# Row sums of a 64 MiB matrix on one core: which rows the first and the last loads of a partition take

## The chip, the core and the metric

The kernel runs on one core of a Trainium2 chip. The metric is the device time of one execution in microseconds, as the median of several runs; lower is better. The profile is of one further execution, and its span begins at the first instruction and ends with the last.

## The reference

```python
batch, seq, dim = 32, 512, 1024
x = np.random.randn(batch, seq, dim).astype(np.float32)

def reference(x):
    return np.sum(x, axis=-1).astype(np.float32)
```

There are 16,384 rows of 1,024 floats (4 KB each), and each row gives one float: 67.1 MB are read, and 64 KB are written.

## The kernel before

Each of the 128 partitions sums J = 128 rows. The rows of the matrix are cut in two regions. `x_a` is the first 2,048 rows, of which partition p takes the 16 rows from 16p on (64 KB from one partition to the next). `x_b` is the other 14,336 rows, of which partition p takes the 112 rows from 2048 + 112p on (448 KB from one partition to the next). The sums stand in one tile `sums` of 128 columns: columns 0 to 111 belong to `x_b`, columns 112 to 127 to `x_a`. `rows_from(j, n)` gives the n rows that belong to the columns from j on, for all partitions. Each load has 128 contiguous runs, one for each partition.

All loads are issued by SyncE in one queue, in this order: a first load of 7 rows for each partition (columns 0 to 6, from `x_b`); seven whole loads of 16 rows, of which the first takes `x_a` (columns 112 to 127) and the six others take `x_b` from column 16 on; then the last 9 rows (columns 7 to 15, from `x_b`) in pieces of 6 rows, 2 rows, 560 floats and 464 floats of the last row. The tiles come from a pool of three buffers, so that a load waits until the reduction of the third tile before it has been done. The first load's instruction is moved to the very start of the program (`issue_first_load_at_entry`). The second load waits until a small ScalarE instruction (`ready`) is over, and the third until the first reduction is done.

VectorE reduces the first load and six whole tiles with one `tensor_reduce` each (line 152). The last whole tile and the pieces are shared between VectorE (`halves`, line 166, which adds the two halves of a row and accumulates) and ScalarE (line 179). At the end ScalarE's queue stores the columns 16 to 111 and the columns 112 to 127 in two DMAs; both wait for the load of the 2 rows. SyncE stores the columns 0 to 15 when the last row is summed. All three stores are issued in line 202, and the end of the program waits for them.

Of the kernel before, what the change touches and what calls it, by code (L numbers as in the profile page):

```python
# [100 lines left out]
@with_exitstack  # L101
def kernel(
    ctx: ExitStack,
    tc: tile.TileContext,
    x: bass.AP,
    out: bass.AP,
):
    nc = tc.nc
    nc.at_finalize(issue_first_load_at_entry)
    nc.at_finalize(order_waits)  # L110
    nc.at_finalize(wait_for_the_store_at_the_clear)
    fp32 = mybir.dt.float32
    P = 128
    batch, seq, dim = x.shape
    rows = batch * seq
    J = rows // P
    BIG = 16

    LONG = J - BIG
    rows_in = x.flatten_outer_dims()
    rows_out = out.rearrange("b s -> (b s)")
    x_a = rows_in[: P * BIG].rearrange("(p j) d -> p j d", p=P)
    x_b = rows_in[P * BIG :].rearrange("(p j) d -> p j d", p=P)
    out_a = rows_out[: P * BIG].rearrange("(p j) -> p j", p=P)
    out_b = rows_out[P * BIG :].rearrange("(p j) -> p j", p=P)


    def rows_from(j, n):
        return x_b[:, j : j + n, :] if j < LONG else x_a[:, j - LONG : j - LONG + n, :]

    last = 0
    FIRST = 7
    pieces = (560, 464)
    LINE = 64

    with (
        tc.tile_pool(name="small", bufs=1) as smallpool,  # L140
        tc.tile_pool(name="in", bufs=3) as inpool,
        tc.tile_pool(name="unread", bufs=4, space=bass.MemoryType.PSUM) as upool,
        tc.tile_pool(name="stage", bufs=1) as stpool,
        tc.manual_schedule(),
    ):


        seed = smallpool.tile([P, LINE // 2], fp32)
        sums = stpool.tile([P, J], fp32)

        def vec(dst, src):
            return nc.vector.tensor_reduce(  # L152
                out=dst, in_=src, axis=mybir.AxisListType.X, op=mybir.AluOpType.add
            )

        def hold(inst, until, reason):
            tc.add_manual_dep(
                inst.ins,
                until.ins.name,
                mybir.DependencyInfo(mybir.DependencyClass.Sync, mybir.DependencyReason.DATA),  # L160
                reason=reason,
            )

        def halves(dst, src):
            n = src.shape[-1] // 2
            return nc.vector.tensor_tensor_reduce(  # L166
                out=src[:, :n],
                in0=src[:, :n],
                in1=src[:, n:],
                scale=1.0,  # L170
                scalar=0.0,
                op0=mybir.AluOpType.add,
                op1=mybir.AluOpType.add,
                accum_out=dst,
            )

        def act(dst, src, n):
            unread = upool.tile([P, dim], fp32)
            nc.scalar.activation(  # L179
                out=unread[:, :n],  # L180
                in_=src,
                func=mybir.ActivationFunctionType.Copy,
                accum_out=dst,
            )

        sums_of = []

        def rows(t, a, n, j, n_act, pairs=False):
            nv = n - n_act
            block = t[:, a * dim : (a + n) * dim].rearrange("p (n d) -> p n d", d=dim)  # L190
            load = nc.sync.dma_start(out=block, in_=rows_from(j, n))  # L191
            if pairs:
                for q in range(nv):
                    sums_of.append(halves(sums[:, j + q : j + q + 1], block[:, q, :]))
            else:
                sums_of.append(vec(sums[:, j : j + nv], block[:, :nv, :]))
            for q in range(nv, n):
                act(sums[:, j + q : j + q + 1], block[:, q, :], dim)
            return load

        def store(eng, dst, j0, j1):
            return eng.dma_start(out=dst, in_=sums[:, j0:j1])

        nc.vector.memset(seed[:, :1], 0.0)  # L204
        unread = upool.tile([P, dim], fp32)
        ready = nc.scalar.activation(  # L206
            out=unread[:, :1], in_=seed[:, :1], func=mybir.ActivationFunctionType.Copy
        )

        j = last  # L210
        t = inpool.tile([P, BIG * dim + LINE], fp32)
        rows(t, 0, FIRST, j, 0)
        first = sums_of[-1]
        wholes = [LONG, *range(BIG, LONG, BIG)]
        for k, at in enumerate(wholes):
            t = inpool.tile([P, BIG * dim + LINE], fp32)
            if k < len(wholes) - 1:
                load = rows(t, 0, BIG, at, 0)
            else:
                rows(t, 0, BIG, at, 7, pairs=True)  # L220
            if k == 0:
                hold(load, ready, "no second load while the first one's descriptors are made")
            if k == 1:
                hold(load, first, "no descriptors of later loads while the first ones start")

        t = inpool.tile([P, BIG * dim + LINE], fp32)
        rows(t, FIRST, 6, j + FIRST, 2, pairs=True)
        two = rows(t, FIRST + 6, 2, j + FIRST + 6, 1, pairs=True)
        a = BIG - 1

        j += a
        c, width = pieces
        whole = t[:, a * dim + c : BIG * dim + 2]
        nc.vector.memset(whole[:, width + 1 :], 0.0)  # L234
        part = t[:, a * dim : a * dim + c]
        nc.sync.dma_start(out=part, in_=rows_from(j, 1)[:, 0, :c])  # L236
        nc.sync.dma_start(out=whole[:, :width], in_=rows_from(j, 1)[:, 0, c:])
        late = "its packets come behind those of the loads"
        hold(store(nc.scalar, out_b[:, BIG:], BIG, LONG), two, late)
        hold(store(nc.scalar, out_a, LONG, J), two, late)  # L240
        halves(whole[:, width : width + 1], part)
        halves(sums[:, j : j + 1], whole)
        store(nc.sync, out_b[:, :BIG], 0, BIG)


# [28 lines left out]
```

## Time and profile before

| what | us |
|---|---|
| median of 3 runs (161.13 to 161.27) | 161.14 |
| span of the profiled execution | 159.5 |
| first load (7 rows) landed | 11.0 |
| one whole tile (16 rows), from landing to landing | 19.3 |
| its `tensor_reduce` on VectorE | 17.2 |
| last piece landed | 157.3 |
| last store issued | 157.8 |

The profiled execution's own time is not listed apart from its span; the median of the runs stands 1.6 us above that span, for what lies around it. The table's times are read from the chain of waits, in order of time, and from the timeline: a reduction starts when its load has landed, so the starts of the reductions give the landings.

### The profile page before, as it was taken

To read this page: it belongs to the slowest core of one execution; us is meant where nothing else is said; L and a number is where in the kernel's file an instruction comes from. 1 tells how busy PE (TensorE), PEld (TensorE's weight loads), DVE (VectorE), ACT (ScalarE), POOL (GpSimd) and SP (SyncE) were. 2 spreads that over 40 slices of the span, in tenths; PEclk is the share of its full clock that TensorE was granted. 3 is DMA by queue.
4 is the path that set the end of the run, shared out by engine and by line. 5 is a ranking of instruction groups with operands and counts; after the bars stand their busy time and mean duration, and the time that the engine had idled before them with its cause. 6 is when DMAs were issued, how large, how long until landed. Compare 5 with 4: busy or idle time off the path is not lost.

```text
span 159.5 us, 135 instructions
## 1 busy us (share of the span) xinstructions
DVE 120.6 (76%) x41; ACT 12.1 (8%) x22; POOL 0.2 (0%) x4
## 2 busy tenths in 40 slices
DVE  0029600499995999769996899949999499994955
ACT  3000000000000000000000000000000000003993
POOL 0000000000000000000000000000000000000000
DMA  8899899699699699699699798996996996996993
GB/s 302 388 493 526 362 427 526 296 493 526 263 526 526 263 526 526 263 526 493 296 526 444 345 526 378 411 526 296 493 526 263 526 526 263 526 526 265 425 382 128
DMA packets 2160, 67.18 MB, mean 421 GB/s; under 512 B 624, under 2 KB 752, under 8 KB 880
## 3 DMA queue, kind: packets, MB, share of 16 engines
q1 hardware_dynamic: 1872, 67.12, 97.8%
q10 hardware_dynamic: 288, 0.06, 0.2%
HBM read 67.11 MB, written 0.07 MB: 421 GB/s over the span
## 4 chain that ended last, share of the span: by engine, by line
DMA 71%; DVE 27%; SPq 1%; issue 0%; DVEq 0%
DMA t<-in_x_dram 71%; DVE sums L152 26%; SPq L191 0%; SPq L236 0%; DVE t L166 0%; DVEq L269 0%
## 5 line engine op out<-in xcount | busy, mean ns | idle before, releaser
L152 DVE TENSOR_REDUCE sums<-t 128x16 f32<-128x16384 f32 (+1 forms) x7 | 110.9, 15849 | 32.3 <-DMA t<-in_x_dram 32.3
L179 ACT ACTIVATE unread<-t 128x1024 f32<-128x1024 f32 x10 | 10.1, 1011 | 144.3 <-DMA t<-in_x_dram 144.3
L166 DVE CUSTOM_DVE_ANT_0 t<-t 128x512 f32<-128x512 f32 (+2 forms) x16 | 9.6, 654 | 4.0 <-DMA t<-in_x_dram 4.0
L179 ACT ACTIVATION_READ_ACCUMULATOR unread<-t 128x1 f32 x10 | 1.9, 188 | 0.0
L206 ACT ACT_TABLE_LOAD x1 | 1.3, 1283 | 0.8 <-PEq L258 0.8
L166 DVE DVE_READ_ACCUMULATOR2_ANT sums<- 128x1 f32 x15 | 1.2, 82 | 0.0
L204 DVE MEMSET seed<- 128x1 f32 x1 | 0.1, 59 | 0.8 <-PEq L258 0.8
L206 ACT ACTIVATE unread<-seed 128x1 f32<-128x1 f32 x1 | 0.2, 174 | 0.0
L258 POOL MEMSET const-bfloat16-1.0<- 128x1 bf16 x1 | 0.1, 102 | 0.0
L258 POOL MEMSET const-uint8-127<- 128x1 uint8 x1 | 0.1, 102 | 0.0
L258 POOL MEMSET const-float32-0.0<- 128x1 f32 x1 | 0.1, 99 | 0.2 <-issue 0.2
L258 POOL MEMSET const-float32-1.0<- 128x1 f32 x1 | 0.1, 99 | 0.0
L166 DVE DVE_READ_ACCUMULATOR2_ANT t<- 128x1 f32 x1 | 0.1, 83 | 0.0
L234 DVE MEMSET t<- 128x1 f32 x1 | 0.1, 59 | 0.0
## 6 DMA issues: line engine op xcount, KB each, us to landing
t<-in_x_dram SPq DMA_DIRECT2D x1, 3584.0 KB, 11.0
t<-in_x_dram SPq DMA_DIRECT2D x1, 3072.0 KB, 28.7
t<-in_x_dram SPq DMA_DIRECT2D x1, 1024.0 KB, 30.7
t<-in_x_dram SPq DMA_DIRECT2D x1, 280.0 KB, 31.0
t<-in_x_dram SPq DMA_DIRECT2D x1, 232.0 KB, 31.1
t<-in_x_dram SPq DMA_DIRECT2D x7, 40.7
out_dram<-sums ACTq DMA_DIRECT2D x1, 48.0 KB, 1.6
out_dram<-sums ACTq DMA_DIRECT2D x1, 8.0 KB, 1.6
```

Source lines behind the costliest of these rows:

```text
L152: return nc.vector.tensor_reduce(out=dst, in_=src, axis=mybir.AxisListType.X, op=mybir.AluOpType.add)
L166: return nc.vector.tensor_tensor_reduce(out=src[:, :n], in0=src[:, :n], in1=src[:, n:], scale=1.0, scalar=0.0, op0=mybir.AluOpType.add, op ...
L179: nc.scalar.activation(out=unread[:, :n], in_=src, func=mybir.ActivationFunctionType.Copy, accum_out=dst,)
L204: nc.vector.memset(seed[:, :1], 0.0)
L206: ready = nc.scalar.activation(out=unread[:, :1], in_=seed[:, :1], func=mybir.ActivationFunctionType.Copy)
L234: nc.vector.memset(whole[:, width + 1 :], 0.0)
L258: nc = _bacc.Bacc("TRN2", target_bir_lowering=False, num_devices=1)
```

## The change

The 16-row region and the 112-row region stay the same rows of the matrix, but other columns and other loads take them. Columns 0 to 15, which are the first load of 7 rows and the last 9 rows, now come from the 16-row region (`near`), and columns 16 to 127, which are the seven whole loads, all come from the 112-row region (`far`). Within the 16-row region, partition 4q+b takes the block of 16 rows with the number 32b+q (before it was partition p and block p). So the partitions 4q, 4q+1, 4q+2 and 4q+3 read blocks 2 MiB apart, and partition 4q+4 reads the block next to that of partition 4q. In the DMA the source of such a load has two counting dimensions (q of 32, then b of 4) and a contiguous run.

The stores follow the loads. ScalarE's queue issues one store of the columns 16 to 127 in place of two, 448 contiguous bytes of each partition, back to back in memory. SyncE's last store writes the columns 0 to 15 as 64-byte runs that together fill 8 KB, in the same order of blocks as the loads; before, its 64-byte runs were 448 bytes apart. The load's target is now written as one contiguous stretch of the tile's row instead of as rows of 1,024.

```diff
-    LONG = J - BIG
+    SPREAD = 4
     rows_in = x.flatten_outer_dims()
     rows_out = out.rearrange("b s -> (b s)")
-    x_a = rows_in[: P * BIG].rearrange("(p j) d -> p j d", p=P)
-    x_b = rows_in[P * BIG :].rearrange("(p j) d -> p j d", p=P)
-    out_a = rows_out[: P * BIG].rearrange("(p j) -> p j", p=P)
-    out_b = rows_out[P * BIG :].rearrange("(p j) -> p j", p=P)
+    near = rows_in[: P * BIG].rearrange("(b q j) d -> q b (j d)", b=SPREAD, j=BIG)
+    far = rows_in[P * BIG :].rearrange("(p j) d -> p (j d)", p=P)
+    out_near = rows_out[: P * BIG].rearrange("(b q j) -> q b j", b=SPREAD, j=BIG)
+    out_far = rows_out[P * BIG :].rearrange("(p j) -> p j", p=P)
+
+    def cols_from(j, c, n):
+        at = j * dim + c
+        return near[:, :, at : at + n] if j < BIG else far[:, at - BIG * dim : at - BIG * dim + n]
 
     def rows_from(j, n):
-        return x_b[:, j : j + n, :] if j < LONG else x_a[:, j - LONG : j - LONG + n, :]
+        return cols_from(j, 0, n * dim)
...
-            load = nc.sync.dma_start(out=block, in_=rows_from(j, n))
+            load = nc.sync.dma_start(out=t[:, a * dim : (a + n) * dim], in_=rows_from(j, n))
...
-        wholes = [LONG, *range(BIG, LONG, BIG)]
+        wholes = range(BIG, J, BIG)
...
-        nc.sync.dma_start(out=part, in_=rows_from(j, 1)[:, 0, :c])
-        nc.sync.dma_start(out=whole[:, :width], in_=rows_from(j, 1)[:, 0, c:])
+        nc.sync.dma_start(out=part, in_=cols_from(j, 0, c))
+        nc.sync.dma_start(out=whole[:, :width], in_=cols_from(j, c, width))
         late = "its packets come behind those of the loads"
-        hold(store(nc.scalar, out_b[:, BIG:], BIG, LONG), two, late)
-        hold(store(nc.scalar, out_a, LONG, J), two, late)
+        hold(store(nc.scalar, out_far, BIG, J), two, late)
         halves(whole[:, width : width + 1], part)
         halves(sums[:, j : j + 1], whole)
-        store(nc.sync, out_b[:, :BIG], 0, BIG)
+        store(nc.sync, out_near, 0, BIG)
```

## The prediction

> **What bounds the kernel now.** I read the page first. Its first line gives the span, and its strip of slices shows the DMA engines busy from the first slice to nearly the last, while VectorE has holes.
>
> ```profile
> span 159.5 us, 135 instructions
> DVE 120.6 (76%) x41; ACT 12.1 (8%) x22; POOL 0.2 (0%) x4
> q1 hardware_dynamic: 1872, 67.12, 97.8%
> HBM read 67.11 MB, written 0.07 MB: 421 GB/s over the span
> ```
>
> The load queue alone holds 97.8% of the 16 engines' time. Next I asked how steady that is: the busy time by windows, each lying inside one whole load.
>
> ```profile
> core 0: us, DVE busy (x) ACT busy (x) POOL busy (x), PEclk, DMA share, GB/s
> 12.00:29.00 17.00, 6.65 (x1) 0.00 (x0) 0.00 (x0) 1.00 1.00 432
> 31.00:48.00 17.00, 16.52 (x1) 0.00 (x0) 0.00 (x0) 1.00 1.00 432
> 128.00:145.00 17.00, 16.12 (x1) 0.00 (x0) 0.00 (x0) 1.00 1.00 432
> ```
>
> The DMA share is 1.00 and the rate 432 GB/s in each of them. The first of these windows reads the 16-row region (64 KB from partition to partition), the others the 112-row region (448 KB); both go at one rate. Only what stands before and after this stream is left to win or lose, so I read the timeline there.
>
> ```profile
> 11.03 7.62 DVE L152 TENSOR_REDUCE sums<-t 128x7 f32<-128x7168 f32 x1 [10.14 <-DMA t<-in_x_dram]
> 30.30 17.22 DVE L152 TENSOR_REDUCE sums<-t 128x16 f32<-128x16384 f32 x1 [11.65 <-DMA t<-in_x_dram]
> 49.62 17.22 DVE L152 TENSOR_REDUCE sums<-t 128x16 f32<-128x16384 f32 x1 [2.10 <-DMA t<-in_x_dram]
> ...
> 146.28 0.69 DVE L166 CUSTOM_DVE_ANT_0 t<-t 128x512 f32<-128x512 f32 x1 [2.16 <-DMA t<-in_x_dram]
> ...
> 156.05 0.94 ACTq L202 DMA_DIRECT2D out_dram<-sums  x2
> ...
> 157.32 0.40 DVE L166 CUSTOM_DVE_ANT_0 t<-t 128x233 f32<-128x233 f32 x1 [0.19 <-DMA t<-in_x_dram]
> 157.65 0.08 DVE L166 DVE_READ_ACCUMULATOR2_ANT sums<- 128x1 f32 x1
> 157.76 0.35 SPq L202 DMA_DIRECT2D out_dram<-sums  x1
> ```
>
> From 30.30 to 146.28 six whole loads of the 112-row region land: 115.98 / 96 = 1.208 us a row. The load of the 16-row region takes 30.30 - 11.03 = 19.27 us, 1.204 a row. VectorE always waits for a landing, some 2.1 us before each tile, so it is never what is late. The first landing is at 11.01 in the chain of waits, where 7 rows at the stream's pace are 8.46: **2.55 us are start**. The 9 last rows take 157.32 - 146.28 = 11.04, against 10.87 at that pace: 0.17 are pieces. From the last landing (157.30) to the end of the span (159.49) 2.19 us pass: the last sum (0.42 with its read-out), the store and the close of the program. The issues by DMA say how long a store takes.
>
> ```profile
> t<-in_x_dram SPq DMA_DIRECT2D x1, 3584.0 KB, 11.0
> out_dram<-sums ACTq DMA_DIRECT2D x1, 48.0 KB, 1.6
> out_dram<-sums ACTq DMA_DIRECT2D x1, 8.0 KB, 1.6
> out_dram<-sums SPq DMA_DIRECT2D x1, 8.0 KB, 1.4
> ```
>
> So before is: start 2.55 + 112 rows at 1.208 (135.30) + 16 rows at 1.204 (19.26) + pieces 0.17 + end 2.19 = 159.47, against 159.49. The median of the runs, 161.14, is 1.65 above that span, and I keep 1.65 for the time around it.
>
> **The change, part by part.**
>
> *The rows that trade places.* The seven whole loads now all read the 112-row region at 1.208: that region still has 112 rows, so 135.30 again. The 16 rows of the other region are now the first 7 and the last 9. Their bytes and runs (28, 24, 8, 2.2 and 1.9 KB for a partition) are as before; only the addresses differ. Nearest line: the same region at 432 GB/s and 1.204. I keep 19.26, so these two edits sum to 0. What this does not show is the new order, in which neighbouring partitions are 2 MiB apart. A bound from above is in the last rival. From below there is next to nothing, since every window inside a whole load has all engines busy at 432.
>
> [...]
>
> *The start.* The first load is issued at 0.00 with nothing ahead of it. Within the first 2 us the DMA view shows only 16 packets, one for each engine, begun near 1.0 us and dense only from there on. [...] First, the source has two counting dimensions. An issue in SyncE's queue takes 0.33 to 0.44 us whatever the load is; if the second dimension doubled that, the packets would come 0.44 later, and by the nearest lines (0.33 for most whole loads, 0.44 for the piece with 1.9 KB runs) a change of shape costs 0 to 0.11. I take +0.05, the middle of these. Second, the engines now start on addresses inside 8 MB instead of over the whole 64 MB. The 1.4 us of the smallest store is the least that any DMA here takes from issue to landing, so the start can fall by 2.55 - 1.4 = 1.15 at most; a loss of the same size is as thinkable. Nothing in the profile gives a sign, and I take 0.
>
> *The last store* is on the path. Its 64-byte runs were 448 bytes apart and now fill 8 KB. The trace has such a store: ScalarE's of 8 KB, packed, lands in 1.6 us beside 1.4 here, but beside the 48 KB store that was issued on the same queue in the same 1.6. Bounds: -0.1 to +0.2 with another 0.35 if the issue of a two-dimensional target doubles. I take 0, by the 48 KB line, which shows no dependence on spacing.
>
> *ScalarE's store.* Two issues (0.94 together, from 156.05) become one: 0.4 to 0.5 less on that queue. Nothing behind them on ScalarE is read by others but the sum whose read-out ends at 157.12, and that runs in the engine beside the queue. SyncE's last store waits for VectorE at 157.73 in any case, and the second of ScalarE's stores lands at the latest near 158.1, a microsecond before SyncE's (157.76 + 1.4 = 159.2). So the gain is 0. If the last store came more than a microsecond sooner, that cover would be gone, and the edit would save up to 0.5.
>
> *The issues of the last four loads* carry the second dimension too. They are made between 124.8 and 126.6 and land 28.7 to 31.1 us later, behind the stream, so a doubled issue (1.6 us more) stays hidden: 0. The next that could be late is the piece itself, which has some 30 us of queued data ahead of it.
>
> Sum: 159.49 + 0.05 + 1.65 = 161.19, so 161.2.
>
> **The rivals.** About 0.2% (0.32 us) is what a measurement of this kernel can tell from no change.
>
> *It does as costed (chance 0.38).* Stream-bound before and after; 160.9 to 161.45.
>
> *The start gets shorter (0.27).* All 16 engines open inside neighbouring blocks, their first packets take less, and the whole stream behind them moves up, since it has no gap to absorb it. The price is up to 1.15; half of it gives 160.6. For it: the start is the only soft stretch, and every tenth there reaches the end. Against it: later packets show no cost of new addresses, as 432 GB/s is held from 12 us on for either layout. It decides when the first reduction starts before 10.7.
>
> *The start and the last store get longer (0.19).* The second counting dimension costs SyncE in two places that nothing covers: 0.33 to 0.44 at the first issue and up to 0.35 at the last. One of them gives 161.5, both 161.9. For it: both stand alone on the path. Against: no issue in the trace varies by more than 0.11 with its shape on SyncE. It decides when the first packets start after 1.3 us, or the last store's issue takes over 0.6.
>
> *The near rows stream slower (0.16).* Engines that read 2 MiB apart hinder one another in memory, or the 32 x 4 split deals the partitions to the engines less evenly. Priced by the lines: at 404 GB/s, the window of 154 to 156 us with its small packets, 16 rows take 16 x 1.208 x 0.07 = 1.3 us more (162.5); at 315, the window of the first 4 us, 7.2 more (168.4); with half the engines 19.3 more (180.5). Against it stands 432 in all windows of both regions, with steps of 64 and of 448 KB. [...]
>
> **How the numbers follow.** Faster by over 0.2% is the shorter start, 0.27; within it is the costed case, 0.38; slower is 0.19 + 0.16 = 0.35. The likeliest single case gives 161.2. Since both signs hold much of the chance, its own range of 160.9 to 161.45 is the narrow one. The range given reaches down to 160.4 (two thirds of the largest gain, which leaves out some 0.04) and up to 162.0 (both issues doubled), and leaves the slower stream outside (0.16).
>
> **What would show each step.** Right: the first reduction starts between 10.8 and 11.3; whole windows stay at 432; the 9 last rows take 11.0 from the last whole landing to the last piece; the last store lands 1.4 after its issue; one issue on ScalarE's queue of 0.4 to 0.5. Wrong: a first reduction before 10.7 or after 11.3, which would shift every later landing by the same amount; a rate clearly under that of before in a window of the near rows (380 GB/s from 4 to 8 us and 410 from 147 to 153 us, where whole packets are booked); a last store over 1.6.

## The result and the profile after

The changed kernel takes 162.09 us (median of 4 runs, 161.99 to 162.16) against 161.20 of the first kernel beside it: a ratio of 1.0053, 95% interval 1.0040 to 1.0065. It is slower by 0.9 us, where 161.2 was forecast and the range ended at 162.0. The span of the profiled execution went from 159.5 to 160.4 us.

The timeline of the changed kernel (start, duration, engine, line, operation; in brackets the idle time before it) shows where the 0.9 us lie.

```profile
11.29 7.62 DVE L156 TENSOR_REDUCE sums<-t 128x7 f32<-128x7168 f32 x1 [9.88 <-DMA t<-in_x_dram]
30.61 17.22 DVE L156 TENSOR_REDUCE sums<-t 128x16 f32<-128x16384 f32 x1 [11.70 <-DMA t<-in_x_dram]
...
146.76 0.69 DVE L170 CUSTOM_DVE_ANT_0 t<-t 128x512 f32<-128x512 f32 x1 [2.20 <-DMA t<-in_x_dram]
...
156.52 0.37 ACTq L206 DMA_DIRECT2D out_dram<-sums  x1
...
157.78 0.40 DVE L170 CUSTOM_DVE_ANT_0 t<-t 128x233 f32<-128x233 f32 x1 [0.17 <-DMA t<-in_x_dram]
158.10 0.08 DVE L170 DVE_READ_ACCUMULATOR2_ANT sums<- 128x1 f32 x1
158.22 0.61 SPq L206 DMA_DIRECT2D out_dram<-sums  x1
```

| stretch | before | after | difference |
|---|---|---|---|
| to the first reduction | 11.03 | 11.29 | +0.26 |
| to the last whole tile | 135.25 | 135.47 | +0.22 |
| the last 9 rows | 11.04 | 11.02 | -0.02 |
| from the last piece to the end of the span | 2.17 | 2.6 | +0.4 |

Two issues on SyncE that nothing covers took longer. The first is the first load's, at 0.0. These lines are the source view of the line that issues the loads, in the window of the first microsecond (durations in ns, least, median and greatest), first of the kernel before, then of the changed one.

```profile
L191 SPq DMA_DIRECT2D t<-in_x_dram x1: 361/361/361, 0.0 to 0.0; - x1
```

```profile
L195 SPq DMA_DIRECT2D t<-in_x_dram x1: 638/638/638, 0.0 to 0.0; - x1
```

The DMA view of the first 2 us has 40 slices of 50 ns; a digit above 0 stands where packets begin. Before and after:

```profile
DMA  0000000000000000000999909990000000000000
```

```profile
DMA  0000000000000000000000000000999909000009
```

The first packets begin in the 20th slice before (1.00 us by the packet records) and in the 29th after (1.44 us). The last store is the other place; the page's list of DMA issues of the changed kernel has issue to landing in its last column.

```profile
t<-in_x_dram SPq DMA_DIRECT2D x1, 3584.0 KB, 11.3
...
out_dram<-sums ACTq DMA_DIRECT2D x1, 56.0 KB, 1.6
out_dram<-sums SPq DMA_DIRECT2D x1, 8.0 KB, 1.8
```

The last store's issue takes 0.61 instead of 0.35, and the store lands 1.8 instead of 1.4 us after its issue began. By the packet records its first packet comes 1.27 us after that moment instead of 0.84: 0.43 later, as at the first load. The stream itself goes at its old rate, by the windows inside the first and the last whole load:

```profile
12.00:29.00 17.00, 6.92 (x1) 0.00 (x0) 0.00 (x0) 1.00 1.00 432
128.00:145.00 17.00, 16.55 (x1) 0.00 (x0) 0.00 (x0) 1.00 1.00 432
```

The +0.22 between the first landing and the last whole tile is too small for these windows to show: in 135 us it would be 0.7 GB/s. The landings of the single engines tell more. A load leaves 16 landings in the trace, which lie 0.46 to 0.63 us from first to last in the loads of the two kernels, and the reduction waits for the last of them (11.27 for the first load, whose reduction begins at 11.29). Averaged over the 16 landings, the first load comes 0.34 us later than before (11.00 against 10.66) and the last piece 0.40 later (157.41 against 157.01): the stream between the two averages grew by 0.06 only, so most of the +0.22 is not a slower stream.

### The profile page after: what moved, and what is told of

Same layout as the page of the kernel before. It is cut to its first block, busy times and chain, and to the rows that moved or that the text cites. A ratio compares the mean times of both kernels' runs of the same rounds, so it can differ in the third digit from the quotient of the medians.

```text
span 160.4 us, 134 instructions
## 1 busy us (share of the span) xinstructions
DVE 120.6 (75%) x41; ACT 12.1 (8%) x22; POOL 0.2 (0%) x4
## 4 chain that ended last, share of the span: by engine, by line
DMA 71%; DVE 26%; SPq 1%; issue 0%; DVEq 0%
DMA t<-in_x_dram 71%; DVE sums L156 26%; SPq L195 1%; SPq L240 0%; DVE t L170 0%; DVEq L272 0%
## 6 DMA issues: line engine op xcount, KB each, us to landing
t<-in_x_dram SPq DMA_DIRECT2D x1, 3584.0 KB, 11.3
```

## The experiments

**Theory A**: a second counting dimension makes an issue on SyncE longer, and that costs in the two places where nothing hides it, at the first load and at the last store. **Theory B**: the addresses cost, that is the near rows first and last, their order of blocks, and the packed store. **Theory C**: part of the loss comes from the whole loads, which all read the far region now.

### One counting dimension again

```diff
-    near = rows_in[: P * BIG].rearrange("(b q j) d -> q b (j d)", b=SPREAD, j=BIG)
+    near = rows_in[: P * BIG].rearrange("(p j) d -> p (j d)", p=P)
-    out_near = rows_out[: P * BIG].rearrange("(b q j) -> q b j", b=SPREAD, j=BIG)
+    out_near = rows_out[: P * BIG].rearrange("(p j) -> p j", p=P)
...
```

> The changed kernel with partition p taking block p of the 16-row region, so that loads and last store have one counting dimension again; region, order of loads and ScalarE's single store stay as changed. Theory A (a second counting dimension lengthens the issue on SyncE, at the first load and the last store): 161.2 us, first landing 11.0, last store 0.35 to issue and 1.4 to land. Theory B (the addresses cost: near rows first and last, all whole loads from the far region, packed store): 162.0, first landing 11.3. Theory C (A for the start and the end, but the 0.2 us that the whole loads lost comes from giving the 16-row region up as a whole load): 161.4.

This kernel is called the plain version below. Measured: 161.37 us against 161.22 (ratio 1.0008, 0.9999 to 1.0017), the first landing at 10.96, the last store 0.35 to issue and 1.4 to land. With the same rows in the same loads, 0.7 of the 0.9 us are gone as soon as the second dimension is. So these 0.7 do not come from where the near rows stand in the order, and not from the packed store. The order of the blocks went away with the dimension here; the two are taken apart below, for the first load. The 0.15 that stays lies at the edge of its interval; theory C is tested below.

### The loads alone, and the store alone

The first kernel of this pair has the plain `out_near` of the diff above and keeps the loads at 32 x 4:

> The changed kernel with only the last store back at one counting dimension (its 8 KB come out in another order of blocks); the loads stay 32 x 4. Theory A: 161.65, that is the changed kernel less 0.45, with a store of 0.35 to issue and 1.4 to land and a first landing at 11.3. Theory B: 162.1 with a store still at 1.8.

The second has the plain `near` and keeps the store at 32 x 4:

> The changed kernel with only the loads back at one counting dimension and the last store left at 32 x 4 (its 8 KB come out in another order of blocks). Theory A: 161.65, the store 0.61 to issue and 1.8 to land, first landing 11.0. Theory B: 162.1, first landing 11.3.

Measured: 161.73 with the loads counted 32 x 4 (ratio to the first kernel 1.0031, 1.0019 to 1.0042) and 161.89 with the store (1.0039, 1.0025 to 1.0053). Against the plain version's 161.37 that is 0.36 for the loads and 0.52 for the store. Here is the last store in the source view and in the list of issues, first of the kernel where only the loads have two dimensions:

```profile
L206 SPq DMA_DIRECT2D out_dram<-sums x1: 356/356/356, 158.2 to 158.2; - x1
```

```profile
out_dram<-sums SPq DMA_DIRECT2D x1, 8.0 KB, 1.4
```

The same two views of the kernel where only the store has:

```profile
L206 SPq DMA_DIRECT2D out_dram<-sums x1: 631/631/631, 157.9 to 157.9; - x1
```

```profile
out_dram<-sums SPq DMA_DIRECT2D x1, 8.0 KB, 1.9
```

The long issue and the late landing go with the store's 32 x 4 target and not with the loads. From the last piece's landing to the store's landing it is 2.31 us in the second kernel and 1.88 in the plain version: +0.43, of which the issue is 0.28. The second kernel's 161.89 is 0.24 over what theory A gave. In its profile the first load, which it leaves alone, lands 0.16 later than in the plain version's (11.12 against 10.96), so the 0.43 is the better figure for the store. The two prices then sum to 0.36 + 0.43 = 0.79 (0.88 by the medians); the step from the plain version to the changed kernel is 162.09 - 161.37 = 0.72, from separate comparisons. Each median is good to about 0.1, and the sum is met no closer than that. No kernel here gives the store a second dimension without a new order of blocks; that its issue grows as the load's does, and its first packet comes later by the same 0.43, speaks for the dimension there, but is not a test.

### 32 x 4 only where it is hidden

```diff
+    near1 = rows_in[: P * BIG].rearrange("(p j) d -> p (j d)", p=P)
...
+        if j == 0:
+            return near1[:, at : at + n]
...
+    out_near = rows_out[: P * BIG].rearrange("(p j) -> p j", p=P)
```

> The changed kernel with one counting dimension at the first load and the last store, and 32 x 4 only in the last four loads, whose issues lie behind 30 us of queued data (the first 7 columns of a partition are then of another block than the last 9). Theory A: 161.2, as the first kernel, though the four issues take 0.6 each. If the 32 x 4 order itself slowed the last 9 rows: over 161.2 by what the time from the last whole landing to the last piece exceeds 11.04.

Measured: 161.40 us (1.0015, 1.0006 to 1.0024), beside 161.37 of the plain version. The four issues took 2.6 us together, from 124.9 to 127.4, and cost nothing that the times show beside the plain version. The last 9 rows took 157.54 - 146.50 = 11.04 from landing to landing, so the 2 MiB steps between neighbouring partitions did not slow them.

### The second dimension without the near rows, and without the new order

The first kernel here is the one before, whose first load counts 32 x 4 over the far region:

```diff
+    x_q = rows_in[P * BIG :].rearrange("(b q j) d -> q b (j d)", b=4, j=LONG)
...
+            if j == 0:
+                load = nc.sync.dma_start(out=t[:, a * dim : (a + n) * dim], in_=x_q[:, :, : n * dim])
...
```

> The kernel before with one edit: the first load still reads the 112-row region, but partition 4q+b takes the first 7 rows of block 32b+q, so its source has two counting dimensions (the first 7 columns then belong to other partitions' rows). Theory A (the second counting dimension costs at the first issue): 161.6, issue 0.64 instead of 0.36, first packets near 1.4 instead of 1.0, first landing 11.3. Theory B (what costs is where the first rows lie): 161.2, first landing 11.0.

The second is the plain version, whose first load counts 32 x 4 at nearly the plain addresses:

```diff
+    step = 4 * BIG + 1
+    dealt = rows_in[: 32 * step].rearrange("(q r) d -> q r d", r=step)
+    dealt = dealt[:, : 4 * BIG, :].rearrange("q (b j) d -> q b (j d)", b=4)
...
+        if j == 0:
+            return dealt[:, :, : n * dim]
```

> The plain version with one edit: the first load counts 32 x 4, at nearly the plain addresses (partition 4q+b reads 7 rows from row 65q+16b on instead of 64q+16b; the first 7 columns belong to rows shifted by up to 31). Theory A: issue 0.64, first packets near 1.4, first landing 11.3, total 161.37 + 0.36 = 161.75, as with only the loads dealt 32 x 4. Theory B (the order of blocks costs, not the count of dimensions): 161.4, first landing 11.0.

Measured: 161.81 (1.0032, 1.0022 to 1.0043) and 161.76 (1.0028, 1.0018 to 1.0037). In the first the issue took 0.62, the first packets began at 1.39 and the first load landed at 11.2; in the second 0.62, and 11.4. The source view has the first load's issue, first of the first kernel, then of the second:

```profile
L194 SPq DMA_DIRECT2D t<-in_x_dram x1: 617/617/617, 0.0 to 0.0; - x1
```

```profile
L201 SPq DMA_DIRECT2D t<-in_x_dram x1: 623/623/623, 0.0 to 0.0; - x1
```

Whether the first load reads near rows 2 MiB apart, near rows in the order of partitions or far rows, it pays for its second dimension: 0.36, 0.39 and 0.6 us by the medians (the ratio of the far one gives 0.52). By the last piece's 16 landings, averaged in the profiled executions, the three are alike, 0.37 to 0.39 later than without the dimension. Theory B is out for the start.

### Other counts

In these two kernels only the constant differs, `SPREAD = 2` and `SPREAD = 8`.

> The changed kernel with SPREAD = 2, so 64 x 2 instead of 32 x 4. Theory A in its plain form (any second counting dimension costs the same): 162.1, issues 0.6. If the cost grows with the inner count: near 161.7.

> The changed kernel with SPREAD = 8, so 16 x 8 instead of 32 x 4. Theory A in its plain form: 162.1, issues 0.6. If the cost grows with the inner count: over 162.6. If the order of blocks matters for the rate of the near rows, the last 9 rows take other than 11.02.

Measured: 162.00 with 64 x 2 (1.0044, 1.0027 to 1.0061) and **181.37** with 16 x 8 (1.1251, 1.1228 to 1.1274). The issue of the first load is 0.66 and 0.64 us, so its cost does not grow with the inner count, and the plain form of theory A holds for 64 x 2. With 64 x 2 neighbouring partitions read blocks 4 MiB apart, and the last 9 rows take 157.77 - 146.72 = 11.05 us, no more than with 32 x 4. The 20 us of 16 x 8 are another thing. Windows of that kernel, in the first load, in a whole load and in the last 9 rows:

```profile
4.00:16.00 12.00, 0.00 (x0) 0.00 (x0) 0.00 (x0) 1.00 0.93 194
31.00:48.00 17.00, 8.58 (x1) 0.00 (x0) 0.00 (x0) 1.00 1.00 432
160.00:175.00 15.00, 3.77 (x13) 5.21 (x10) 0.00 (x0) 1.00 0.96 207
```

The DMA engines are as busy in the near rows as elsewhere (a share of 0.93 and 0.96) and move less than half as much. A packet of 28 KB takes 2.23 us in the median instead of 1.06. The first landing is at 20.3 us instead of 11.3, and the last 9 rows take 21.4 instead of 11.0.

In 16 x 8 neighbouring partitions also stand 1 MiB apart, so one more kernel tells the addresses from the counts: the diff of the plain version above, with `step = 8 * BIG + 1`, 16 and `b=8`, so that only the first load counts 16 x 8, at nearly the plain addresses.

> The plain version (one counting dimension, partition p takes block p) with one edit: the first load counts 16 x 8, at nearly the plain addresses: partition 8q+b reads 7 rows from row 129q+16b on instead of 128q+16b (so the first 7 columns belong to rows shifted by up to 15). If the half pace of SPREAD = 8 comes from the counts (16 x 8 deals the partitions to the engines so that two share something): first landing near 20.3, total near 171. If it came from the 1 MiB between neighbouring partitions: first landing 11.3, total 161.8.

Measured: 170.10 us (1.0545, 1.0519 to 1.0572). The list of issues and a window inside the first load:

```profile
t<-in_x_dram SPq DMA_DIRECT2D x1, 3584.0 KB, 20.1
```

```profile
4.00:18.00 14.00, 0.00 (x0) 0.00 (x0) 0.00 (x0) 1.00 0.96 203
```

The half pace comes with the counts 16 x 8, with blocks 64 KB apart as well as 1 MiB. In both kernels the engines are busy and a packet takes twice as long: here a share of 0.96 of 16 engines over 14 us gives 2.2 us for each of the 99 packets in that window, beside the 2.23 above. Why is not shown: no run here lists which engine wrote which partition, and that two share something, as the text above has it, is the author's guess.

### Without a whole load of the 16-row region

```diff
-            load = nc.sync.dma_start(out=block, in_=rows_from(j, n))
+            load = nc.sync.dma_start(out=block, in_=rows_from(BIG if j == LONG else j, n))
```

> The kernel before, whose first whole load reads rows of the 112-row region (the same as the next whole load's) instead of the 16-row region, so that all seven whole loads read the far region; the 16-row region is not read and its sums are not computed. Theory C (the 0.15 us that the plain version stands above the first kernel come from having no whole load of the 16-row region): 161.35, with 135.4 us from the first landing to the last whole landing. Otherwise: 161.2 and 135.25.

Measured: 161.24 against 161.21 (1.0005, 0.9993 to 1.0017). The stretch from the first landing to the last whole landing became 135.48 us, as theory C said, but the first landing came at 10.71, and the total stood 0.03 above the first kernel's where theory C had 0.14. The runs give theory C no support, though their interval would still hold its 0.14. The stretch between the last landings is not a measure by itself: here the last of the first load's 16 landings came 0.30 us earlier than in the first kernel (10.71 against 11.01) and their average only 0.06 (10.60 against 10.66), and the later stretch is 0.23 longer (135.48 against 135.25) at the same total. What makes the plain version 0.15 us slower than the first kernel, if it is, stays open. The kernel with 32 x 4 in the hidden loads stands as high (161.40), which makes mere chance less likely.

## Why the prediction was wrong

- **The step that failed** is the term "+0.05" for the second counting dimension at the start, and the 0 for it at the last store. The first issue took 0.28 longer, its packets came 0.44 later, and the time for that is about 0.4 us instead of 0.05. The last store took 0.27 longer to issue and 0.42 longer to land, and its time is 0.43 (0.52 by the medians) instead of 0. I had taken the middle of 0 and 0.11 from lines that all had one counting dimension. No line of the profile had a second one, and a price between such lines could not hold it.
- **The 0.11 was misread** besides. I took 0.33 and 0.44 for different shapes. In the profile of before the third and the fourth load are both whole loads; the third's issue takes 0.33 and the fourth's, begun 0.05 us behind it, 0.43. The difference goes with issues back to back, not with their shape.

```profile
L191 SPq DMA_DIRECT2D t<-in_x_dram x2: 328/377/426, 18.7 to 19.1; - x2
```

- **The rival that came true** is the longer start and last store, given a chance of 0.19 and 161.9. Its mechanism and both places were right. Its price was an issue that doubles; the issue rose by a factor of 1.77 instead, but from the end of the issue to the first packet another 0.16 passed at each place. With that and the open 0.15, the range's end at 162.0 was 0.1 short. "Against: no issue varies by more than 0.11 with its shape" was the misreading that kept its chance low. Of the signs named for it, the first packets after 1.3 us (1.44) and the last store's issue over 0.6 (0.61) came true; the general sign for the start, a first reduction after 11.3, was set too wide and missed it by 0.01 (11.29).
- **The rows that trade places**, taken as 0: right in the stream (432 GB/s in each whole load, 11.02 instead of 11.04 for the last 9 rows), with at most the open 0.15. Rows 2 MiB apart from partition to partition moved at the old pace.
- **The packed last store**, taken as 0: right. In the plain version 64-byte runs side by side land in 1.4 us, as they did 448 bytes apart.
- **ScalarE's one store**, taken as 0: right. It saves 0.57 us on that queue (0.37 instead of 0.94) and nothing in the time.
- **The hidden issues**, taken as 0: right, by the kernel that has only those.
- **The shorter start** (0.27) did not come: first packets in the near region took 1.06 to 1.95 us in the changed and the plain kernel, against 1.53 to 2.11 before. But first packets from the far region took 1.06 to 1.94 and 1.19 to 1.89 in two other kernels, so this is not the region, and the plain version's first load landed only 0.05 us earlier than before (10.96 against 11.01).
- **The slower near rows** (0.16) did not come at 32 x 4 either (11.02 us for the last 9 rows against 11.04). The price of the bound "half the engines", 180.5, is near what 16 x 8 measures as 181.37, but there all engines are at work (a share of 0.93 to 0.96), at half their pace (194 to 207 GB/s).

No kernel of these runs beats the first one.

## What to carry to other kernels

Count the dimensions of a DMA's access pattern before counting its bytes. In these runs an issue whose source or target needs two counting dimensions costs some 0.3 us more on its queue (0.62 to 0.66 against 0.36 at the first load) and 0.4 us until data moves or lands; that was free behind 30 us of queued data (161.40 against 161.37 us) and fully paid at the first load and the last store (0.36 and 0.52 us by the medians). When a profile has no line of the kind that a change brings, the small gaps between the lines that it has do not bound the price, and the rival that needs such a line deserves a larger chance. A partition order written as 16 x 8 instead of 32 x 4 halved the rate of the loads here with all engines busy (194 to 207 GB/s at a share of 0.93 to 0.96, against 432), so look at GB/s beside the share.

## What was not expected of the hardware

- An issue on SyncE with two counting dimensions takes 0.54 to 0.67 us, whether 64 x 2, 32 x 4 or 16 x 8, load or store; with one it takes 0.33 to 0.39, and 0.42 to 0.48 right behind another.
- Where the first load has two counting dimensions, ScalarE and VectorE start later too: ScalarE's first instruction begins at 1.25 to 1.31 us instead of 0.76 to 0.80, VectorE's at 1.32 to 1.38 instead of 0.84 to 0.86. Here that costs nothing: the second load, which waits for ScalarE, is issued at 2.8 instead of 2.3 us, long before the first load lands at 11.
- Loads to 128 partitions ran at 432 GB/s with counts of 128, and the 9 last rows at their old pace with 32 x 4 (11.02 us, 11.04 before); with 16 x 8 the rate was 194 to 207 GB/s at a DMA share of 0.93 to 0.96.
- The last of the first load's 16 landings came 0.3 us earlier in one kernel without moving the end (10.71 against 11.01, and 161.24 against 161.21 us; averaged over the 16 the landing is at 10.60 against 10.66): average over the landings before a difference of tenths is put down to a stretch.
